# Weight columns in rows of 512: the end of each encoder layer computed by token instead of by feature

## The chip, the cores and the metric

The kernel runs on one core of a Trainium2 chip. Times are device microseconds of one execution; three executions of the kernel before are given with their median. A profile is one execution of its own, with a record of every instruction of the engines: TensorE (PE for its matmuls, PEld for its weight loads), VectorE (DVE), ScalarE (ACT), GpSimd (POOL) and the queue that issues the transfers (SP).

## The reference

A trunk of two layers works on 256 tokens of 1024 features in float32. Each layer computes

```
h = rmsnorm(x, norm_g[l])
proj = h @ w_in[l]                       # inputs of three mixers, their gate paths, 3 x 1024 merge logits
y_a = hgrn2(...) * silu(a_g)             # 1024 wide
y_b = retention(...) * silu(b_g)         # 2048 wide
y_c = rwkv7(...) * silu(c_g)             # 1024 wide
gates = sigmoid(merge)                   # 3 x 1024 per token
mixed = gates[0] * (y_a @ w_branch_a[l]) + gates[1] * (y_b @ w_branch_b[l]) + gates[2] * (y_c @ w_branch_c[l])
x = x + mixed @ w_out[l]
```

and after the last layer a final rmsnorm gives the output. The change concerns the last three lines: merge gates, branch products, output projection. Here they are called the tail of a layer.

## The kernel before, in words

All large products are made in a split form. A weight piece of 128 partitions and 1024 values (512 KB) is loaded (`wr`, in `load_w`), ScalarE casts it to float32r (`wh`, L184), and VectorE takes the difference (`wl`, L187). The other operand has a high and a low part as well (`h_hi` and `h_lo`, `yh` and `yl`, `m_hi` and `m_lo`), and three matmuls stand for one product: high times high, high times low, low times high. `wr`, `wh` and `wl` have three buffers each, which the pieces take in turn.

A block of weights is 1024 rows and 256 columns, which is two pieces. There are two ways to use one:

- `feat_mm` (L200): features on the output's partitions. The stationary operand is a 128 x 128 tile of the weights, the moving one all 256 tokens. A piece holds 128 columns of the block, and 24 matmuls use it.
- `tok_mm` (L210): tokens on the output's partitions. The stationary operand is a 128 x 128 tile of the activations, the moving one 256 weight columns. A piece holds four of the eight k-tiles; the token tile is the outer loop, so both pieces of a block are in use until its second half.

The three mixers come first. Their products are mixed on TensorE with small plain float32 matmuls of the scans (`c_o`, `c_oc`, `b_o`, `b_t` and others). Function `tail` then runs three branches (m = 0, 1, 2 for A, B, C) with four blocks each (b = 0 to 3). For a block, `proj` computes the gate logits into a PSUM bank `pj` (tile `p_mg`), ScalarE and VectorE make the sigmoid in `t_g`, `feat_mm` accumulates the branch product in two half banks of tag `c` (tile `t_o`; branch B takes two weight blocks), VectorE multiplies by the gate (L770), and GpSimd adds to the accumulator `t_acc` (L772). In the last branch the sum is cast to `m_hi` and `m_lo` (L779, L780), with features on the partitions as the output projection needs it for its stationary operand. The output projection, four blocks `wo` by `tok_mm` into `pj`, is added to x (L793), and ScalarE sums the squares for the next norm (L794). `load_y` fetches the mixers' outputs from DRAM through one buffer `yr` and splits them.

The order of the instructions on each engine is written at build time by a planner that simulates the program; instructions of the tail may stand among the last scan's. Each engine's queue runs in that order. PSUM has eight banks: two `pj`, two `c`, two `n`, one `s`, one `ab`.

In SBUF the mixers' tiles lie at bytes 78,848 to 192,000 of a partition (the scan C, with `c_os` as the topmost) and 192,704 to 229,336 (A and B, 35.8 KB). The tail's pool `early` (`t_acc`, `t_g`, `yh0`, `yl0`, `yr`; 34 KB) lies at 194,528 to 229,344, with `t_acc` at its lower end; a tile there waits for the earlier tiles under it.

Of the kernel before, what the change touches and what calls it, by code (L numbers as in the profile page):

```python
# [8 lines left out]
F32 = mybir.dt.float32  # L9
F32R = mybir.dt.float32r  # L10
# [10 lines left out]
NBLK = 93  # L21
WS = (1024, 1024)
TOK = ("ai", "bv", "wo")
# [9 lines left out]
# columns of a layer's packed parameters  # L33
# [9 lines left out]
# columns of the shape constants  # L43
# [9 lines left out]
# of the masks that A takes, and of the rotation that B takes  # L53
# [4 lines left out]
# blocks of weights in a layer, in the order of _blocks()  # L58
# [3 lines left out]
def _blocks():  # L62
    """(key, matrix, row range start, list of (column start, width)) of each block of 1024 rows and 256 columns."""
# [13 lines left out]
    for m in range(3):  # L77
        for b in range(4):
            c = 256 * b
            r.append((("mg", m, b), "w_in", 0, [(15616 + 1024 * m + c, 256)]))  # L80
            for n, w, r0 in ((("wa", "w_branch_a", 0),), (("wb0", "w_branch_b", 0), ("wb1", "w_branch_b", 1024)),
                             (("wc", "w_branch_c", 0),))[m]:
                r.append(((n, b), w, r0, [(c, 256)]))
    for b in range(4):
        r.append((("wo", b), "w_out", 0, [(256 * b, 256)]))
# [3 lines left out]
for _i, _b in enumerate(_blocks()):  # L89
    BK[_b[0]] = _i  # L90
assert len(BK) == NBLK


@with_exitstack
def trunk(ctx: ExitStack, tc, x, wb, pp, lora, cst, gtab, ng, out, parts="ABCT", layers=L, dbg=None):
# [10 lines left out]
    # x and what its norm takes come before the other constants  # L106
# [36 lines left out]
    DP = []  # L143
    for l in range(L):
# [3 lines left out]
        # 1 - mu0 - mu1  # L148
# [7 lines left out]
    # lower bounds: softmax over the layers with its maximum, cumulated, less the first  # L156
# [13 lines left out]
    # cumsum - p[0]  # L170
# [6 lines left out]
    def load_w(l, key):  # L177
        """the parts of a block's halves"""
        W = []
        for h in range(2):  # L180
            raw = ring(wp, [128, 1024], F32, "wr", RW[0], "wr")
            nc.sync.dma_start(raw, wb[2 * (l * NBLK + BK[key]) + h])
            hi = ring(wp, [128, 1024], F32R, "wh", RW[1], "wh")
            S.copy(hi, raw)  # L184
            lo = ring(wp, [128, 1024], F32R, "wl", RW[2], "wl")
            n = WS[h]
            V.tensor_sub(lo[:, 0:n], raw[:, 0:n], hi[:, 0:n].bitcast(F32))  # L187
            if n < 1024:
                G.tensor_sub(lo[:, n:], raw[:, n:], hi[:, n:].bitcast(F32))
            W.append((hi, lo))  # L190
        return W
# [11 lines left out]
    def tok_mm(o, W, t, h):  # L203
        """o[t, column] = h[:, t-tile]^T W; a half of the block holds four k-tiles"""
# [25 lines left out]
    def silu_from(pool, src, shape, tag, tmp, bufs=1, tb=1):  # L230
        """silu of a projection in PSUM"""
# [8 lines left out]
    def norm_T(xs, ss, gb, pool):  # L240
        """xs and the sums of its squares by token; gb: the gains, on every partition"""
# [53 lines left out]
    def c_codes(l, pool):  # L295
# [3 lines left out]
        # tanh(x) = 2 sigmoid(2 x) - 1  # L299
# [5 lines left out]
    def c_prep(l, p, codes, pool):  # L305
        """Everything of pair p up to the chunk products, evacuated and masked."""
# [13 lines left out]
        # normalised kk, negated  # L320
# [8 lines left out]
        # decay and a  # L329
# [21 lines left out]
        # its ninth block holds the stacked identity  # L351
# [4 lines left out]
        # bonus: sum of r k_d r_k over both directions  # L356
# [7 lines left out]
        # k~, beta~, alpha~, r~ of each direction, and the products within its chunks  # L364
# [6 lines left out]
        for d in range(2):  # L371
            # a chunk's blocks of 64: A_rk^T, r~, A_ak, A_rb^T, beta' (first alpha~), A_ab^T, k', diag g, alpha~^T
# [30 lines left out]
    def c_solve(l, p, st, pool):  # L403
        """Inverses of the diagonal 32 x 32 blocks of I - A_ab, one block and every fourth column a partition."""
# [17 lines left out]
        # inverses of the diagonal 4 x 4 blocks, in place: entry (i, k) of block I at 132 I + 32 k + i  # L422
# [27 lines left out]
    def c_scan(l, p, st, pool, ydst):  # L450
# [10 lines left out]
        # v of each direction, transposed  # L461
# [18 lines left out]
        # (I - A_ab)^-1 [A_ak, alpha~^T] by blocks of 32, for a direction's four chunks at a time  # L480
# [14 lines left out]
        # what a chunk makes of its v and of the state before it: mt its output, mk the state after it  # L495
# [19 lines left out]
        # the state from chunk to chunk  # L515
# [24 lines left out]
        # group norm over a head's 64 partitions  # L540
# [14 lines left out]
    # ================= A: HGRN2 =================  # L555
    def a_pair(l, p, pool, ydst):
# [6 lines left out]
        # k = (1 - lb) sigmoid(-x), f = lb + (1 - lb) sigmoid(x); the first layer's lb is p[0] - p[0] = 0  # L563
# [28 lines left out]
    def a_head(l, hd, le, kq, v, g, pool, ydst):  # L592
        # decay sums within 128 positions: forward, and backward negated
# [10 lines left out]
        def pairs(e, s):  # L604
            """K (lower forward, upper backward) and Q (lower backward, upper forward), scaled"""
# [6 lines left out]
        # between the two tiles of 128  # L612
# [30 lines left out]
        # within 8 positions, from their middle  # L643
# [16 lines left out]
        # output, its norm over the 128 partitions and the gate  # L660
# [27 lines left out]
    # ================= B: retention =================  # L688
# [52 lines left out]
    # ================= merge and output =================  # L741
# [10 lines left out]
    def tail(l, ya, yb, yc, x_src, early, pool):  # L752
        acc = [early.tile([128, 2, T], F32, name=f"t_acc{b}") for b in range(4)]
        Y, xs = [], None
        for m in range(3):
            br = ((("wa", 0),), (("wb0", 1), ("wb1", 2)), (("wc", 3),))[m]
            for b in range(4):
# [4 lines left out]
                if b == 0:  # L762
                    Y += [load_y(src, early, pool if m else early, n) for src, n in (((ya, 0),), ((yb[:, 0:8], 1), (yb[:, 8:16], 2)), ((yc, 3),))[m]]
                o = [ps.tile([128, 256], F32, tag="c", bufs=PB["c"], name="t_o") for f in range(2)]
# [180 lines left out]
```

## Time and profile before

| | |
|---|---|
| Runs | 1819.37, 1821.67, 1822.58 us; median 1821.67 |
| Profiled execution | span 1821.9 us from the first to the last instruction; no other time of this execution is recorded |
| Granted TensorE clock, mean | 0.965 |
| Tail of layer 0 | first gate matmul at 695.3 us, last addition of the output projection done at 905.2 us |
| Tail of layer 1 | end at 1821.9 us, with the final norm |
| Weight pieces | 372 transfers of 512 KB, 3.3 us from issue to landing |

A line of the groups reads: source line, engine, operation, output <- inputs, shape, count | busy us, mean ns of one | idle time of the engine just before them, and what ended it. A line of the chain of work reads: start, duration, engine or DMA, output, line, count. A line of the timeline reads: start, duration, engine, line, operation, operands. Durations of matmuls are those of one from start to end and overlap; the distance between starts is what a matmul costs in a stream.

### The profile page before, as it was taken

To read this page: it belongs to the slowest core of one execution; us is meant where nothing else is said; L and a number is where in the kernel's file an instruction comes from. 1 tells how busy PE (TensorE), PEld (TensorE's weight loads), DVE (VectorE), ACT (ScalarE), POOL (GpSimd) and SP (SyncE) were. 2 spreads that over 40 slices of the span, in tenths; PEclk is the share of its full clock that TensorE was granted. 3 is DMA by queue.
4 is the path that set the end of the run, shared out by engine and by line. 5 is a ranking of instruction groups with operands and counts; after the bars stand their busy time and mean duration, and the time that the engine had idled before them with its cause. 6 is when DMAs were issued, how large, how long until landed. Compare 5 with 4: busy or idle time off the path is not lost.

```text
span 1821.9 us, 33791 instructions
## 1 busy us (share of the span) xinstructions
PE 1667.6 (92%) x12960; PEld 1625.0 (89%) x12960; DVE 1415.4 (78%) x2597; ACT 1056.5 (58%) x1940; POOL 322.0 (18%) x312
## 2 busy tenths in 40 slices
PE   6888899999999999999888789988999999999997
PEld 6877899898999998999888788988889999999997
DVE  5799898998878785565657989989998787846554
ACT  5665566757465545555556556757573656456453
POOL 1122222212120200010011222223131202100100
PEclk9989999999999999999988889999999999999999
DMA  6333223324344443755533233233244444437653
GB/s 221 116 118 105 79 96 102 117 86 138 119 155 141 146 148 133 244 200 187 198 114 118 99 100 91 88 109 107 93 133 125 144 142 154 142 131 245 208 186 116
DMA packets 127873, 250.30 MB, mean 137 GB/s; under 512 B 62304, under 2 KB 66784, under 8 KB 127456
## 3 DMA queue, kind: packets, MB, share of 16 engines
q1 hardware_dynamic: 127712, 248.15, 41.6%
q8 instruction: 102, 1.67, 0.4%
q14 instruction: 59, 0.48, 0.1%
HBM read 229.22 MB, written 14.68 MB: 134 GB/s over the span
## 4 chain that ended last, share of the span: by engine, by line
PE 49%; DVE 30%; issue 7%; DMA 6%; ACT 4%; SPq 2%; POOL 0%; DVEq 0%; ACTq 0%; POOLq 0%
PE t_o L200 10%; PE p_mg L200 8%; DVE wl L187 7%; DVE c_tq L439 3%; PE p_bv L210 3%; PE p_vg L200 3%; PE p_bg L200 2%; DMA c_M<-s 2%; PE pj L210 2%; PE c_p L393 2%; DMA s<-c_Z 2%; ACT wh L184 2%; DVE c_ts L441 2%; PE p_rk L200 1%; PE c_p L395 1%
## 5 line engine op out<-in xcount | busy, mean ns | idle before, releaser
L187 DVE TENSOR_TENSOR wl<-wr,wh 128x1024 fp32r<-128x1024 f32 x372 | 475.9, 1280 | 192.3 <-ACT wh L184 190.9
L184 ACT CAST wh<-wr 128x1024 fp32r<-128x1024 f32 x372 | 388.4, 1045 | 272.7 <-PE t_o L200 56.2
L200 PE MATMUL t_o<-yh,wh 128*128 128x256 f32 x512 | 144.7, 284 | 2.8 <-ACT yh L748 2.8
L200 PE MATMUL t_o<-yl,wh 128*128 128x256 f32 x512 | 145.0, 284 | 0.5 <-DVE yl L749 0.5
L200 PE MATMUL t_o<-yh,wl 128*128 128x256 f32 x512 | 144.6, 283 | 0.0
L608 POOL TENSOR_TENSOR a_sl<-a_kq,a_e 128x256 f32<-128x256 f32 x80 | 80.9, 1015 | 230.9 <-ACT a_e L618 66.0
L200 PE MATMUL p_mg<-h_hi,wh 128*128 128x256 f32 x384 | 109.6, 285 | 0.0
L200 PE MATMUL p_mg<-h_hi,wl 128*128 128x256 f32 x384 | 109.4, 285 | 0.0
L200 PE MATMUL p_mg<-h_lo,wh 128*128 128x256 f32 x384 | 108.7, 283 | 0.0
L200 PEld LDWEIGHTS t_o<-yh,wh 128*128 128x128 f32 x512 | 97.6, 191 | 3.2 <-ACT yh L748 3.2
L200 PEld LDWEIGHTS t_o<-yl,wh 128*128 128x128 f32 x512 | 97.9, 191 | 1.0 <-DVE yl L749 0.9
L200 PEld LDWEIGHTS t_o<-yh,wl 128*128 128x128 f32 x512 | 97.9, 191 | 0.0
L393 PE MATMUL c_p<-c_Z,bbd 128*128 128x192 f32 x256 | 68.9, 357 | 29.7 <-DVE bbd L388 25.0
L439 DVE TENSOR_TENSOR c_tq<-W,c_M 128x16 f32<-128x16 f32 (+6 forms) x112 | 89.0, 795 | 1.4
L200 PE MATMUL p_vg<-h_hi,wh 128*128 128x256 f32 x256 | 78.1, 305 | 8.1 <-ACT c_k L288 4.1
L399 ACT COPY c_Z<-c_p 128x192 f32<-128x192 f32 x128 | 40.3, 318 | 74.9 <-DVE c_Z L396 73.7
L200 PE MATMUL p_bg<-h_hi,wl 128*128 128x256 f32 x256 | 75.0, 293 | 4.6 <-DVE wl L187 4.6
L210 PE MATMUL p_bv<-wh,h_hi 128*128 128x256 f32 x256 | 76.1, 297 | 1.1 <-ACT b_z L694 1.1
L210 PE MATMUL p_bv<-wl,h_hi 128*128 128x256 f32 x256 | 75.4, 295 | 1.7 <-DVE wl L187 1.7
L200 PE MATMUL p_vg<-h_lo,wh 128*128 128x256 f32 x256 | 75.8, 296 | 0.0
L200 PE MATMUL p_vg<-h_hi,wl 128*128 128x256 f32 x256 | 75.6, 295 | 0.0
L210 PE MATMUL p_bv<-wh,h_lo 128*128 128x256 f32 x256 | 74.7, 292 | 0.0
(334 smaller groups left out, 5983.3 us busy)
## 6 DMA issues: line engine op xcount, KB each, us to landing
wr<-in_wb_dram SPq DMA_DIRECT2D x372, 512.0 KB, 3.3
c_M<-s SPq DMA_DIRECT2D x64, 128.0 KB, 2.7
c_lt<-in_lora_dram SPq DMA_DIRECT2D x16, 256.0 KB, 2.7
b_sw<-b_z SPq DMA_DIRECT2D x16, 256.0 KB, 3.9
b_gt<-in_gtab_dram SPq DMA_DIRECT2D x16, 256.0 KB, 3.4
yb<-b_y SPq DMA_DIRECT2D x16, 256.0 KB, 3.0
yr<-yb SPq DMA_DIRECT2D x8, 512.0 KB, 5.0
s<-c_Z SPq DMA_DIRECT2D x128, 16.0 KB, 1.9
```

The costliest lines, as they stand in the source:

```text
L184: S.copy(hi, raw)
L187: V.tensor_sub(lo[:, 0:n], raw[:, 0:n], hi[:, 0:n].bitcast(F32))
L200: PE.matmul(o, a[:, k], b[:, k, :], start=(first and n == 0), stop=(last and n == 3 * KT - 1))
L210: PE.matmul(o, a[:, k, t * 128:(t + 1) * 128], b, start=(n == 0), stop=(n == 3 * KT - 1))
L393: PE.matmul(o[:, 2:5], bbd[:, c], z[:, c, 1:8:3], start=True, stop=True)
L395: PE.matmul(o[:, 0:6:5], kbd[:, c], z[:, c, 1:8:6], start=True, stop=True)
L399: S.copy(z[:, c, 4:9:2], o[:, 4:7])
L439: V.tensor_mul(tp, W[:, 0:n, None, 0:j].to_broadcast([128, n, 4, j]), M[:, 0:j, j:j + 4].rearrange("p j i -> p i j")[:, None].to_broadcast ...
L441: V.tensor_reduce(sm, tp, axis=AX.X, op=ALU.add)
L608: G.tensor_mul(s5[:, :, :, 0], k5[:, 0:2, :, 0], e5[:, :, :, 0])
```

## The change

In the tail a block of weights becomes 1024 rows and 512 columns, four pieces of two k-tiles each. The stationary operand of all three products is now a 128 x 128 tile of the activations, the moving one 512 weight columns, and each of the two token tiles has a PSUM bank of its own. Both `pj` banks hold one block of gate logits, both `c` banks one block of a branch product. `t_acc` and `t_g` are by token, 2 x 512 values per partition. The finished sum is transposed on TensorE, four 128 x 128 tiles to a bank of tag `n`, and split into `m_hi` and `m_lo` from there. The number of pieces, transfers, casts and differences stays. The mixers' own products are unchanged. Comments are dropped throughout.

```diff
+    def load_half(l, key, h):
+        raw = ring(wp, [128, 1024], F32, "wr", RW[0], "wr")
+        nc.sync.dma_start(raw, wb[l * NHLF + BK[key] + h])
+        hi = ring(wp, [128, 1024], F32R, "wh", RW[1], "wh")
+        S.copy(hi, raw)
+        lo = ring(wp, [128, 1024], F32R, "wl", RW[2], "wl")
+        V.tensor_sub(lo, raw, hi.bitcast(F32))
+        return hi, lo
...
+    def wide_mm(o, l, key, h, first=True, last=True):
+        hhi, hlo = h
+        for c in range(4):
+            whi, wlo = (w.rearrange("p (k c) -> p k c", c=512) for w in load_half(l, key, c))
+            for i in range(2):
+                k = 2 * c + i
+                for t in range(2):
+                    r = slice(t * 128, (t + 1) * 128)
+                    for n, (a, b) in enumerate(((hhi, whi), (hlo, whi), (hhi, wlo))):
+                        PE.matmul(o[t], a[:, k, r], b[:, i], start=(first and k == 0 and n == 0),
+                                  stop=(last and k == KT - 1 and n == 2))
...
     def tail(l, ya, yb, yc, x_src, early, pool):
-        acc = [early.tile([128, 2, T], F32, name=f"t_acc{b}") for b in range(4)]
+        acc = [early.tile([128, 2, 512], F32, name=f"t_acc{n}") for n in range(2)]
...
-            for b in range(4):
-                o = proj(l, ("mg", m, b))
-                g = early.tile([128, 2, T], F32, tag="t_g", bufs=TG, name="t_g")
-                S.activation(g, o, AF.Exp, scale=-1.0)
+            for n in range(2):
+                o = two("pj", "p_mg")
+                wide_mm(o, l, ("mg", m, n), (h_hi, h_lo))
+                g = early.tile([128, 2, 512], F32, tag="t_g", bufs=TG, name="t_g")
+                for t in range(2):
+                    S.activation(g[:, t], o[t], AF.Exp, scale=-1.0)
                 sigmoid_of_exp(g)
...
-                    W = load_w(l, (key, b))
-                    for f in range(2):
-                        feat_mm(o[f], W, f, Y[y], first=(i == 0), last=(i == len(br) - 1))
-                for f in range(2):
-                    V.tensor_mul((g if m else acc[b])[:, f], o[f], g[:, f])
-                if m:
-                    G.tensor_add(acc[b], acc[b], g)
+                    wide_mm(o, l, (key, n), Y[y], first=(i == 0), last=(i == len(br) - 1))
+                for t in range(2):
+                    V.tensor_mul((g if m else acc[n])[:, t], o[t], g[:, t])
+                    if m:
+                        G.tensor_add(acc[n][:, t], acc[n][:, t], g[:, t])
...
-                    S.copy(m_hi[:, 2 * b:2 * b + 2], acc[b])
-                    V.tensor_sub(m_lo[:, 2 * b:2 * b + 2], acc[b], m_hi[:, 2 * b:2 * b + 2].bitcast(F32))
+                    for t in range(2):
+                        o = ps.tile([128, 4, 128], F32, tag="n", bufs=PB["n"], name="t_t")
+                        for k in range(4):
+                            PE.transpose(o[:, k], acc[n][:, t, 128 * k:128 * k + 128], ident)
+                        hi = m_hi[:, 4 * n:4 * n + 4, 128 * t:128 * t + 128]
+                        S.copy(hi, o)
+                        V.tensor_sub(m_lo[:, 4 * n:4 * n + 4, 128 * t:128 * t + 128], o, hi.bitcast(F32))
...
-        for b in range(4):
-            W = load_w(l, ("wo", b))
-            o = ring(ps, [128, 2, 256], F32, "pj", PB["pj"], "pj")
-            r = slice(256 * b, 256 * b + 256)
-            for t in range(2):
-                tok_mm(o[:, t], W, t, (m_hi, m_lo))
-            for t in range(2):
-                sq = pool.tile([128, 256], F32, tag="t_sq", bufs=2, name="t_sq")
-                V.tensor_add(xs[:, t, r], xs[:, t, r], o[:, t])
-                S.activation(sq, xs[:, t, r], AF.Square, accum_out=s4[:, t, b:b + 1])
+        for n in range(2):
+            o = two("pj", "pj")
+            wide_mm(o, l, ("wo", n), (m_hi, m_lo))
+            r = slice(512 * n, 512 * n + 512)
+            for t in range(2):
+                sq = pool.tile([128, 512], F32, tag="t_sq", bufs=2, name="t_sq")
+                V.tensor_add(xs[:, t, r], xs[:, t, r], o[t])
+                S.activation(sq, xs[:, t, r], AF.Square, accum_out=s4[:, t, n:n + 1])
```

More of the change, by code (lines that the diff above doesn't have):

```diff
@@ L20 @@
 KT = D // 128
-NBLK = 93
-WS = (1024, 1024)
-TOK = ("ai", "bv", "wo")
+NHLF = 186
+TOK = ("ai", "bv")
+WIDE = ("mg", "wa", "wb0", "wb1", "wc", "wo")
 PB = {"pj": 2, "c": 2, "n": 2, "s": 1, "ab": 1}
@@ L77, in _blocks @@
     for m in range(3):
-        for b in range(4):
-            c = 256 * b
-            r.append((("mg", m, b), "w_in", 0, [(15616 + 1024 * m + c, 256)]))
-            for n, w, r0 in ((("wa", "w_branch_a", 0),), (("wb0", "w_branch_b", 0), ("wb1", "w_branch_b", 1024)),
+        for n in range(2):
+            c = 512 * n
+            r.append((("mg", m, n), "w_in", 0, [(15616 + 1024 * m + c, 512)]))
+            for k, w, r0 in ((("wa", "w_branch_a", 0),), (("wb0", "w_branch_b", 0), ("wb1", "w_branch_b", 1024)),
                              (("wc", "w_branch_c", 0),))[m]:
-                r.append(((n, b), w, r0, [(c, 256)]))
-    for b in range(4):
-        r.append((("wo", b), "w_out", 0, [(256 * b, 256)]))
-    return r
-for _i, _b in enumerate(_blocks()):
-    BK[_b[0]] = _i
-assert len(BK) == NBLK
+                r.append(((k, n), w, r0, [(c, 512)]))
+    for n in range(2):
+        r.append((("wo", n), "w_out", 0, [(512 * n, 512)]))
+    return r
+_o = 0
+for _b in _blocks():
+    BK[_b[0]] = _o
+    _o += 4 if _b[0][0] in WIDE else 2
+assert _o == NHLF
 @with_exitstack
@@ L174, in trunk @@
     V.tensor_scalar(omlb, lb, -1.0, 1.0, op0=ALU.mult, op1=ALU.add)
-    def load_w(l, key):
[L179 to L191, printed above, removed]
+    def load_half(l, key, h):
[6 more added lines that the diff above has]
+        return hi, lo
+    def load_w(l, key):
+        return [load_half(l, key, h) for h in range(2)]
+    def wide_mm(o, l, key, h, first=True, last=True):
[9 more added lines that the diff above has]
+                                  stop=(last and k == KT - 1 and n == 2))
     def feat_mm(o, W, f, h, first=True, last=True):
@@ L752, in tail, with two @@
     def tail(l, ya, yb, yc, x_src, early, pool):
-        acc = [early.tile([128, 2, T], F32, name=f"t_acc{b}") for b in range(4)]
+        acc = [early.tile([128, 2, 512], F32, name=f"t_acc{n}") for n in range(2)]
         Y, xs = [], None
+        def two(tag, name):
+            return [ps.tile([128, 512], F32, tag=f"{tag}{t}", bufs=1, name=name) if tag == "pj" else
+                    ps.tile([128, 512], F32, tag=tag, bufs=PB[tag], name=name) for t in range(2)]
         for m in range(3):
@@ L756, in tail @@
             br = ((("wa", 0),), (("wb0", 1), ("wb1", 2)), (("wc", 3),))[m]
-            for b in range(4):
-                o = proj(l, ("mg", m, b))
-                g = early.tile([128, 2, T], F32, tag="t_g", bufs=TG, name="t_g")
-                S.activation(g, o, AF.Exp, scale=-1.0)
+            for n in range(2):
+                o = two("pj", "p_mg")
[3 more added lines that the diff above has]
+                    S.activation(g[:, t], o[t], AF.Exp, scale=-1.0)
@@ L761, in tail @@
                 sigmoid_of_exp(g)
-                if b == 0:
-                    Y += [load_y(src, early, pool if m else early, n) for src, n in (((ya, 0),), ((yb[:, 0:8], 1), (yb[:, 8:16], 2)), ((yc, 3),))[m]]
-                o = [ps.tile([128, 256], F32, tag="c", bufs=PB["c"], name="t_o") for f in range(2)]
+                if n == 0:
+                    Y += [load_y(src, early, pool if m else early, i) for src, i in (((ya, 0),), ((yb[:, 0:8], 1), (yb[:, 8:16], 2)), ((yc, 3),))[m]]
+                o = two("c", "t_o")
@@ L778, in tail @@
                         m_lo = pool.tile([128, KT, T], F32R, name="m_lo")
-                    S.copy(m_hi[:, 2 * b:2 * b + 2], acc[b])
-                    V.tensor_sub(m_lo[:, 2 * b:2 * b + 2], acc[b], m_hi[:, 2 * b:2 * b + 2].bitcast(F32))
-        s4 = pool.tile([128, 2, 4], F32, name="t_s4")
+                    for t in range(2):
[5 more added lines that the diff above has]
+                        V.tensor_sub(m_lo[:, 4 * n:4 * n + 4, 128 * t:128 * t + 128], o, hi.bitcast(F32))
+        s4 = pool.tile([128, 2, 2], F32, name="t_s4")
         ss = pool.tile([128, 2], F32, name="t_ss")
@@ L890, in _pack @@
     a = {k: np.asarray(v) for k, v in inputs.items()}
-    wb = np.empty((L * NBLK, 2, 128, 1024), np.float32)
+    wb = np.empty((L * NHLF, 128, 1024), np.float32)
     for l in range(L):
-        for n, (key, mat, r0, cols) in enumerate(_blocks()):
+        for key, mat, r0, cols in _blocks():
             m = np.concatenate([a[mat][l, r0:r0 + 1024, c0:c0 + w] for c0, w in cols], 1)
+            n = l * NHLF + BK[key]
+            if key[0] in WIDE:
+                wb[n:n + 4] = m.reshape(4, 2, 128, 512).transpose(0, 2, 1, 3).reshape(4, 128, 1024)
+                continue
             if key[0] in TOK:
```

8 lines of the change are left out of this document (4 added, 4 removed).

## The prediction

> **What bounds the kernel now.** First the page's first block and the windows, to see which engine is full in the part that changes (the tail of each layer: gates, branch products, output projection); then the chain of work, to see whether anything but TensorE sets its pace; then the groups, for counts.
>
> ```profile
> PE 1667.6 (92%) x12960; PEld 1625.0 (89%) x12960; DVE 1415.4 (78%) x2597; ACT 1056.5 (58%) x1940; POOL 322.0 (18%) x312
> ...
> 740.00:780.00 40.00, 40.00 (x336) 39.95 (x336) 24.71 (x27) 25.20 (x31) 1.48 (x2) 1.00 0.77 268
> 820.00:860.00 40.00, 40.00 (x335) 40.00 (x335) 23.87 (x26) 20.92 (x25) 3.87 (x3) 1.00 0.52 183
> 880.00:890.00 10.00, 8.74 (x70) 8.33 (x70) 5.54 (x6) 3.62 (x7) 0.83 (x1) 1.00 0.45 158
> ```
>
> A window row reads: length, then busy time and instructions of PE, PEld, DVE, ACT, POOL, then the granted clock, the DMA share, GB/s. From 740 to 880 us TensorE is never idle at full clock, VectorE is at 60%, ScalarE at 52 to 63%. Busy alone doesn't prove a bound, since matmul records overlap; the chain does:
>
> ```profile
> 758.04 5.68 PE t_o L200 x48
> 763.73 5.75 PE p_mg L200 x48
> 769.47 11.52 PE t_o L200 x96
> ...
> 873.15 5.65 PE t_o L200 x47
> 878.83 1.06 ACT wh L184
> 879.91 2.02 DVE wl L187
> 881.97 3.52 PE pj L210 x27
> ```
>
> The chain runs through TensorE alone for 140 us: 96 matmuls in 11.52 us, 120 ns each, block after block. Only the output projection (`pj`) has weight waits on it. So the tail's time is the number of matmuls times their spacing, and the change is about that product. The counts:
>
> ```profile
> L200 PE MATMUL t_o<-yl,wh 128*128 128x256 f32 x512 | 145.0, 284 | 0.5 <-DVE yl L749 0.5
> L200 PE MATMUL p_mg<-h_hi,wh 128*128 128x256 f32 x384 | 109.6, 285 | 0.0
> L210 PE MATMUL pj<-wl,m_hi 128*128 128x256 f32 x128 | 36.6, 286 | 2.5 <-DVE wl L187 2.5
> ```
>
> Each is one of three equal groups: 3 x (512 + 384 + 128) = 3072 matmuls of 256 columns. (The mean of 284 ns is the latency of one; the spacing is 120.) At 120 ns they are 368.6 us of the 1821.9.
>
> **Term 1: 3072 matmuls of 256 columns become 1536 of 512.** The work in columns stays; halved are the instructions and weight loads. The gain therefore hangs on why 256 columns take 120 ns. The timeline, PEld and PE rows in turn:
>
> ```profile
> 788.03 0.19 PEld L200 LDWEIGHTS t_o<-yl,wh 128*128 128x128 f32 x1
> 788.15 0.19 PEld L200 LDWEIGHTS t_o<-yh,wl 128*128 128x128 f32 x1
> ...
> 1788.04 0.28 PE L200 MATMUL t_o<-yh,wh 128*128 128x256 f32 x1
> 1788.16 0.28 PE L200 MATMUL t_o<-yl,wh 128*128 128x256 f32 x1
> ```
>
> Loads and matmuls alternate, both every 120 ns. The chain's rows of the mixers show what other shapes cost (plain float32):
>
> ```profile
> 688.33 0.22 PE c_oc L521 x2
> ...
> 698.47 1.73 PE b_o L718 x8
> ...
> 703.66 0.89 PE c_o L486 x8
> ...
> 706.51 0.44 PE b_t L732 x4
> ```
>
> `c_oc` has 64 columns and costs 0.22 / 2 = 110 ns; `c_o` has 128 and costs 0.89 / 8 = 111; `b_o` has 256 and costs 1.73 / 8 = 216. From 64 to 128 columns nothing is added: the weight load sets a floor of about 111. From 128 to 256 it adds 105, so there the stream sets the time, and the load hides behind it. A plain float32 column takes twice the stream of a float32r one (256 float32r columns take 120, 256 float32 ones 216), so `b_o` is the nearest row to 512 float32r columns with a new weight tile each time: 216. I read 120 as the load's floor, just above the 105 or so that 256 float32r columns need. Bounds for the new matmul: below, 216 (the stream of `b_o`); above, 240, two of today's, if 120 is all streaming; between them, 120 + 105 = 225, if the excess is a fixed sum per instruction. I take 216, since `b_o` has the same alternation of load and stream: 1536 x 216 = 331.8 us, **-36.8**.
>
> The Trainium skill, TensorE: Matmul & The Clock Gate, section Back-to-back issue gap, gives N / 2.4 + 2.5 ns for an isolated warm matmul: 216 at 512 columns, as `b_o`, but 109 at 256, where the trace has 120; by it alone term 1 would be an estimated 1536 x (218 - 216) = 3 us and the time near rival (c)'s. The trace disagrees at 256 columns, and the 120 measured there decides. The same section says that the spacing of load and matmul pairs is set by both operations, which is the reading above and what the trace's floor of 111 bears out.
>
> **Term 2: the transposes.** Sixteen 128x128 transposes a layer, in four groups of four. The row of `b_t` is such a group among other matmuls: 0.44 us with its switches. 8 x 0.44 = **+3.5**. The copies out of them replace the old casts, four of 512 columns a layer before and after:
>
> ```profile
> L253 ACT CAST h_hi<-n_t x8: 586/586/589, 12.8 to 912.9; 128x512 fp32r<-128x512 f32 x8
> L779 ACT CAST m_hi<-t_acc x8: 620/621/622, 846.3 to 1790.5; 128x512 fp32r<-128x512 f32 x8
> L780 DVE TENSOR_TENSOR m_lo<-t_acc,m_hi x8: 677/678/679, 847.3 to 1791.5; 128x512 fp32r<-128x512 f32 x8
> ```
>
> From PSUM 586 against 620: nothing.
>
> **Term 3: the chain from the last branch product to the output projection.**
>
> ```profile
> 1788.60 0.42 DVE L770 TENSOR_TENSOR t_g<-t_o,t_g 128x256 f32<-128x256 f32 x1 [0.29 <-PE t_o L200]
> 1789.19 1.29 POOL L772 TENSOR_TENSOR t_acc<-t_acc,t_g 128x512 f32<-128x512 f32 x1 [10.23 <-DVE t_g L770]
> ```
>
> Today: product, GpSimd add, cast, difference (m_lo starts 1791.5, 0.68 long: 3.6 us in all), hidden by the first matmuls of `pj`. After: two products of 512 columns (0.68 each by the m_lo row), two adds one after the other (2 x 1.29), transposes 0.44, cast 0.59, difference 0.68: 0.68 + 2.58 + 0.44 + 0.59 + 0.68 = 5.0, with semaphores about 5.8 (today 0.6 of the 3.6 are such). The cover is the first half of `wo` block 0, k-tiles 0 to 3, which need only the first 512 columns of the sum: 24 matmuls, 5.2 us. Uncovered 0.5 a layer: **+1**. That holds if TensorE's order has those matmuls before the last transposes; its queue is in order, and if the transposes stand first, it waits for 0.68 + 2.58 = 3.3 us a layer, 6.5 in all. The order on TensorE here already puts later matmuls between the earlier ones' waits (`p_mg` around `c_o`), so I take the small value.
>
> **Term 4: the output projection's waits.** Today its two token tiles each run through both half-blocks, so both halves are released late:
>
> ```profile
> PE pj L210 <- DVE wl L187: 1.3, 2, 0.7
> PE t_o L200 <- ACT yh L748: 1.4, 1, 1.4
> ```
>
> That is 1.3 us a layer. After, each 512 KB piece is used by 12 matmuls and released: **-2.6**. In exchange both `pj` banks belong to one 512-column block, and block 1 waits for block 0's additions. The add of token tile 0 (0.68) runs beside tile 1's last three matmuls (0.65), so about 0.5 a layer: **+1**. At the very end tile 0's add begins 0.65 earlier and both take longer (0.68 against 0.42): nothing.
>
> **Term 5: the start of the tail, beside the last scan.** Three things move. The gates need both `pj` banks at once; one is held until the last `b_pair` has read it:
>
> ```profile
> L236 DVE TENSOR_TENSOR s_g<-p_bg,s_tmp x1: 692/692/692, 699.6 to 699.6; 128x512 f32<-128x512 f32 x1
> 695.54 0.71 PE p_mg L200 x6
> 696.68 1.78 PE p_mg L200 x15
> 740.46 1.06 PE p_mg L200 x9
> 745.73 0.33 SPq L553 DMA_DIRECT2D yc<-c_os  x1
> yc<-c_os SPq DMA_DIRECT2D x16, 128.0 KB, 2.2
> ```
>
> So the 21 matmuls that ran between 695.5 and 698.5 lose their place: 2.5 us. Against that, one gate block is now 48 x 216 = 10.4 us of filler instead of 5.8, beside the 1.4 us in which TensorE waited for `yh` and others like it. Third, `t_g` grows from 2 to 4 KB in three buffers; the pool `early` from 34 to 40 KB, downward. It lay within the 35.8 KB that A and B had left; now the first accumulator reaches under the last scan's tiles, `c_os` the last of them, free when the store issued at 745.7 lands (2.2 us). Today two gate blocks and two products are done by 740, when the third gate block starts; so the first 512 block's product is due there and may wait some 8 us, with a gate block (10.4 us) in between as cover, provided that VectorE's queue has the weight differences ahead of it. I take **+1** a layer for the three, between -1.5 (filler wins) and +5 (VectorE is blocked): **+2**.
>
> **Term 6: the weight feed.** The pieces, 512 KB each, are the same 372, on SP's queue in nearly the same order; `load_y` follows four pieces instead of two. TensorE takes one in 12 x 216 = 2.6 us instead of 2.88. A buffer's round is landing, cast, difference:
>
> ```profile
> wr<-in_wb_dram SPq DMA_DIRECT2D x372, 512.0 KB, 3.3
> L187 DVE TENSOR_TENSOR wl<-wr,wh 128x1024 fp32r<-128x1024 f32 x50 | 66.4, 1329 | 46.2 <-ACT wh L184 46.1
> L184 ACT CAST wh<-wr 128x1024 fp32r<-128x1024 f32 x51 | 53.4, 1048 | 56.4 <-PE t_o L200 28.0 <-PE p_mg L200 24.4 <-DMA wr<-in_wb_dram 4.0
> ```
>
> 3.3 + 1.05 + 1.33 = 5.7 over three buffers is 1.9 a piece, under 2.6, and the casts wait for TensorE, not it for them. Where `yb` is read as well, 268 GB/s become some 295 at a share of 0.85: **+1** for that. ScalarE's and VectorE's sigmoid work is the same elements in half the instructions, off the path.
>
> **Sum.** -36.8 + 3.5 + 1 - 2.6 + 1 + 2 + 1 = -30.9. The profiled span of 1821.9 lies 0.2 above the median of the runs (1821.67); 1821.9 - 30.9 = **1791**.
>
> **Rivals.** (a) *A fixed sum per instruction*: 225 ns a matmul, 345.6 us, 14 more: **1805**. For it: no float32r row of another width; against it: `b_o` has no such excess over the stream. (b) *New waits*: transposes ahead of `wo` (+5.5) and the first accumulator blocking VectorE (+8): between 1796 and 1805, say **1802**. For it: in-order queues and both banks taken at once; against it: the slack of a gate block. (c) *The other side: float32r streams at 120 ns per 256 columns*. Then 512 cost 240, term 1 is nothing, and the new work remains: 1821.9 + 5.9 = **1828**. It decides from (368.6 - 5.9) / 1536 = 236 ns a matmul upward. For it: 120 is above both the floor of 111 and the stream of 105. Against it: blocks with pauses run below 120, as this one, at 2.02 / 17 = 119, and a stream bound would not give back.
>
> ```profile
> 725.32 2.02 PE t_o L200 x17
> ```
>
> (d) *The price is per instruction*, whatever the columns: 1536 x 120, a gain of 184: **1643**. Against it: `c_o` to `b_o`, where columns double and so does the price. The Trainium skill, in the section named, gives about 131 ns as the sustained spacing at 512 columns; by it 1536 x 131 would be an estimated gain of 167. The trace bears out nothing of that. (e) *The planner's new order disturbs the scans* and eats the gain: **1818**.
>
> **Chances.** Forecast 0.60 (own range 1783 to 1798), (a) 0.14, (b) 0.13, (c) 0.08, (d) 0.01, (e) 0.04. 1783 to 1810 holds the forecast's cases and (a) and (b) but for their tails. 0.2% (3.6 us) is about what a measurement tells from no change: faster 0.88, same 0.03, slower 0.09.
>
> **What would show it.** Right: groups of `t_o` x256, `p_mg` x192, `pj` x64 with 128x512, and 48 of them in 10.4 us on the chain; `pj` waits for VectorE gone; four transposes at 0.44. 10.8 means (a), 11.5 means (c). A gap of 3 us before the transposes or one near 740 to 748 means (b). The prediction falls if the spacing is over 225 or TensorE's idle time in the tail grows by more than 5 us a layer.

## The result, and the profile after

The change made the kernel slower: 1849.18 us median (four runs, 1844.83 to 1854.19) against 1820.52 for the kernel before in the same session (1815.17 to 1822.58), a ratio of 1.0166 with a 95% interval of 1.0141 to 1.0192. The forecast was 1791 with a range up to 1810; the error is 58 us. The profiled execution took 1854.19 us with a span of 1852.4; a span is 1.7 to 2.4 us, mostly 1.8, shorter than the time of its execution in every run here that has both.

First the stretches that the prediction argued from, by the windows of both kernels: from the first gate matmul to the last matmul of the output projection, layer 0 and layer 1. Columns: window, length, busy time and count of PE, PEld, DVE, ACT, POOL, granted clock, DMA share, GB/s. Before:

```profile
695.30:903.73 208.43, 203.89 (x1687) 202.10 (x1685) 120.49 (x145) 111.99 (x155) 15.53 (x13) 1.00 0.56 192
1605.37:1813.35 207.98, 203.46 (x1685) 201.77 (x1683) 118.74 (x143) 109.13 (x151) 15.54 (x13) 1.00 0.53 181
```

After:

```profile
698.07:918.43 220.36, 202.41 (x935) 165.63 (x933) 115.59 (x124) 107.89 (x135) 18.43 (x13) 0.96 0.58 181
1624.41:1843.83 219.42, 201.35 (x933) 164.05 (x930) 113.07 (x122) 105.13 (x131) 18.35 (x13) 0.97 0.54 172
```

The two tails together went from 416.4 to 439.8 us, +23.4. (The whole profiled execution is 30.5 us longer; the other 7.1 us lie outside the tails, and what they are due to is not shown.) Length less PE's busy time is idle TensorE: 4.5 us a layer before, 18 after. Where it is idle, and for what, stands in TensorE's waits of layer 0's tail:

```profile
PE t_o L202 <- ACT yh L760: 11.0, 1, 11.0
...
PE c_ox L517 <- ACT qp L514: 2.2, 2, 1.3
```

One wait of 11.0 us, for the high part of `ya`. The chain of work of after, at that place and then in the steady part (start, duration, what):

```profile
734.90 0.71 PE c_gn L557 x2
...
738.53 0.73 POOL c_os L564
739.27 0.33 SPq L565
739.65 5.74 DMA yr<-ya
...
795.16 21.76 PE t_o L202 x96
816.92 10.88 PE p_mg L202 x48
...
877.22 0.44 PE t_t L800 x4
...
894.04 5.44 PE pj L202 x24
899.48 0.89 PE t_t L800 x8
900.37 1.22 DVE wl L186
901.59 0.61 DVE m_lo L803
```

Two things are to be read here. First, the chain runs from the scan's last normalisation over the store of `yc` (L565) straight into the first load of `ya`: the whole tail hangs behind the scan. From there to 791.6, where rows are left out, the chain is the eight loads of `load_y`, one after another through the one buffer `yr`, each with its cast and difference; from 746.6 to 791.0 TensorE is busy beside them for all but 0.6 us. Second, the new stream: 96 matmuls in 21.76 us, 48 in 10.88, that is 227 ns each, where the forecast took 216. The queue that issues transfers, in the kernel before:

```profile
710.29 0.42 SPq L747 DMA_DIRECT2D yr<-ya  x1
718.69 0.32 SPq L747 DMA_DIRECT2D yr<-ya  x1
724.65 0.32 SPq L747 DMA_DIRECT2D yr<-yb  x1
745.73 0.33 SPq L553 DMA_DIRECT2D yc<-c_os  x1
750.34 0.33 SPq L747 DMA_DIRECT2D yr<-yb  x1
```

and after:

```profile
704.20 0.33 SPq L565 DMA_DIRECT2D yc<-c_os  x1
739.27 0.33 SPq L565 DMA_DIRECT2D yc<-c_os  x1
739.65 0.42 SPq L759 DMA_DIRECT2D yr<-ya  x1
```

Before, three loads go out ahead of the last store of `yc`, and branch A's products fill TensorE beside the last scan. After, the first goes out behind that store, 29 us later. Between the first gate matmul and 735.6 us, TensorE had two gate blocks and 60 product matmuls of 256 columns to put beside the scan in the kernel before, and has one gate block (48 matmuls of 512 columns) and no product in after. The rest of what used to fill the scan's pauses is still to be done when it ends.

### The profile page after: what moved, and what is told of

It is laid out like the page before. It is cut to its first block, busy times and chain, and to the rows that moved or that the text cites. A ratio compares the mean times of both kernels' runs of the same rounds, so it can differ in the third digit from the quotient of the medians.

```text
span 1852.4 us, 30668 instructions
## 1 busy us (share of the span) xinstructions
PE 1662.5 (90%) x11456; PEld 1548.0 (84%) x11456; DVE 1407.7 (76%) x2553; ACT 1048.7 (57%) x1900; POOL 324.2 (18%) x312
## 4 chain that ended last, share of the span: by engine, by line
PE 43%; DVE 32%; DMA 10%; issue 7%; ACT 5%; SPq 2%; POOL 1%; DVEq 0%; ACTq 0%; POOLq 0%
PE t_o L202 7%; DVE wl L186 7%; PE p_mg L202 5%; PE p_bv L222 3%; DVE c_tq L451 3%; PE p_vg L212 2%; PE pj L202 2%; PE p_bg L212 2%; DMA c_M<-s 2%; PE p_rk L212 2%; DMA yr<-yb 2%; DVE c_ts L453 2%; PE c_p L405 2%; DMA s<-c_Z 1%; ACT wh L184 1%
## 5 line engine op out<-in xcount | busy, mean ns | idle before, releaser
L202 PE MATMUL t_o<-wh,yh 128*128 128x512 f32 x256 | 101.1, 398 | 21.3 <-ACT yh L760 21.3
L202 PE MATMUL t_o<-wh,yl 128*128 128x512 f32 x256 | 101.6, 397 | 0.1
L202 PE MATMUL t_o<-wl,yh 128*128 128x512 f32 x256 | 92.2, 395 | 0.0
L790 POOL TENSOR_TENSOR t_acc<-t_acc,t_g 128x512 f32<-128x512 f32 x16 | 28.2, 1788 | 289.4 <-DMA wr<-in_wb_dram 156.5
L202 PE MATMUL p_mg<-wh,h_hi 128*128 128x512 f32 x192 | 75.8, 395 | 2.4 <-ACT wh L184 2.4
L202 PEld LDWEIGHTS t_o<-wh,yh 128*128 128x128 f32 x256 | 48.7, 191 | 32.5 <-ACT yh L760 22.1
L202 PE MATMUL p_mg<-wh,h_lo 128*128 128x512 f32 x192 | 75.2, 391 | 0.0
L212 PE MATMUL p_bg<-h_lo,wh 128*128 128x256 f32 x256 | 74.9, 292 | 0.0
L212 PE MATMUL p_bg<-h_hi,wh 128*128 128x256 f32 x256 | 74.6, 292 | 0.0
L212 PE MATMUL p_rk<-h_hi,wh 128*128 128x256 f32 x256 | 74.5, 291 | 0.0
```

The source lines that it names most:

```text
L202: PE.matmul(o[t], a[:, k, r], b[:, i], start=(first and k == 0 and n == 0), stop=(last and k == KT - 1 and n == 2))
L212: PE.matmul(o, a[:, k], b[:, k, :], start=(first and n == 0), stop=(last and n == 3 * KT - 1))
L790: G.tensor_add(acc[n][:, t], acc[n][:, t], g[:, t])
```

## The experiments

Each kernel was timed beside the kernel before. The time is the median; the ratio is against the kernel before, with its interval. "Tails" is the sum of the two tails' lengths, "idle" the part of it without a busy TensorE, both from window rows like those above, of one profiled execution. Where the granted clock is lowered, the busy part is longer for it. In e8, e10 and e11 something of the computation is left out, as their expectations say.

| Kernel | Time, us | Ratio | Tails, us | Idle, us |
|---|---|---|---|---|
| before | 1820.2 to 1820.9 | | 416.4 | 9.1 |
| after | 1849.18 | 1.0166 (1.0141 to 1.0192) | 439.8 | 36.0 |
| e1: second accumulator moved | 1828.19 | 1.0046 (1.0030 to 1.0062) | 421.0 | 19.6 |
| e2: before with a pool of 40 KB | 1861.73 | 1.0221 (1.0195 to 1.0248) | 451.8 | 34.7 |
| e3: accumulators swapped | 1840.13 | 1.0109 (1.0075 to 1.0143) | 434.8 | 32.7 |
| e4: only the output projection wide | 1816.69 | 0.9975 (0.9959 to 0.9990) | 412.3 | 7.1 |
| e5: e1 with two raw buffers, two gate buffers | 1830.11 | 1.0050 (1.0035 to 1.0066) | 421.9 | 19.6 |
| e6: both accumulators moved, two raw buffers | 1838.00 | 1.0094 (1.0071 to 1.0118) | 427.2 | 24.1 |
| e7: before with two raw buffers, two gate buffers | 1826.72 | 1.0039 (1.0024 to 1.0055) | 416.9 | 8.0 |
| e8: e1, each matmul split to 256 | 1816.70 | 0.9987 (0.9970 to 1.0003) | 412.4 | 3.4 |
| e9: mixed, branch A narrow | 1817.41 | 0.9984 (0.9970 to 0.9998) | 408.3 | 9.7 |
| e10: e9 without transposes | 1806.89 | 0.9927 (0.9909 to 0.9945) | 403.8 | 7.7 |
| e11: only branch A wide | 1826.31 | 1.0033 (1.0017 to 1.0050) | 421.4 | 10.1 |

### The reach of the pool: e1, e2, e3

Theory M: the pool `early` grew from 34 to 40 KB and now begins at 188,384, so that its lowest tile, the first accumulator, lies over tiles of the scan (which end at 192,000). The accumulator must wait for them, and the planner then puts the loads behind the scan's last store. e1 takes 4 KB out of `early`; the rest ends above the scan:

```diff
-        acc = [early.tile([128, 2, 512], F32, name=f"t_acc{n}") for n in range(2)]
+        acc = [(early, pool)[n].tile([128, 2, 512], F32, name=f"t_acc{n}") for n in range(2)]
```

> The changed kernel with one of its two accumulators (t_acc1, 4 KB) moved from the pool `early` to the tail's other pool; nothing else differs. `early` is then 36 KB and no longer reaches under the last scan's tiles. Theory M (memory: the lower end of `early` under the scan's tiles makes the planner hold back the whole start of the tail): the first load of ya is issued near 712 us instead of 739.7, the 11 us wait of t_o for yh shrinks to under 3, and with 1536 matmuls at 227 ns instead of 3072 at 120 (-20) and some 6 us of new work the time is 1820.5 - 14 = about 1806, range 1798 to 1814. Rival B (banks: both PSUM banks taken at once and a block twice as long leave TensorE without other work beside the scan): the wait stays, and the time is that of the changed kernel, 1849, at most 5 us less.

e2 puts the harm into the kernel before, with its tiling untouched, by nothing but buffers that are not needed:

```diff
-TG, YR = 3, 1
+TG, YR = 6, 1
```

> The kernel before with six buffers for t_g instead of three (12 KB, as the changed kernel has for it); nothing else differs, and the three more buffers are not needed. Its pool `early` is then 40 KB, as in the changed kernel, and lies under the last scan's tiles as there. Theory M: the first load of ya is issued only after the last store of yc, near 740 us, and TensorE waits for yh as in the changed kernel: +15 to +25 us a layer, 1850 to 1870. Rival B: no 512-column block and no pair of banks is here, so the time stays within 4 us of 1820.5.

e3 leaves the pool at 40 KB and puts the second accumulator, which is needed later, at its lower end:

```diff
-        acc = [early.tile([128, 2, 512], F32, name=f"t_acc{n}") for n in range(2)]
+        acc = [early.tile([128, 2, 512], F32, name=f"t_acc{1 - n}") for n in range(2)][::-1]
```

> The changed kernel with the two accumulators exchanged in the pool: the one that lies under the scan's tiles is now that of the second 512 columns, first written some 20 us later, when the scan's last tile is free. Theory M in the form W (the first write to the accumulator waits for the scan's tiles): the wait is gone, 1806 to 1815. Theory M in the form O (the planner gives the pool's tiles out in program order and holds back all later ones behind the one that has to wait, whichever is written first): as the changed kernel, 1849 within 5 us.

e2 shows that M is real: 41 us slower. (Three more gate buffers come with the larger pool; that they do harm by themselves is not tested apart from it.) Its waits and its transfer queue are those of after:

```profile
PE t_o L200 <- ACT yh L748: 11.9, 2, 10.4
...
728.28 0.33 SPq L553 DMA_DIRECT2D yc<-c_os  x1
728.66 0.42 SPq L747 DMA_DIRECT2D yr<-ya  x1
```

e1 takes back 21 of after's 28.7 us, and its first load goes out at 708.4 again; but it ends 7 us behind the kernel before, not 14 ahead as M alone forecast. e3 keeps the late load (issued at 728.97, right behind the store at 728.60) and a wait of 10.3 us for `yh`, though the tile that reaches into the scan's memory is not written before the second product: so what delays the loads is the order that the planner writes, not a wait of the first product. That is form O, but its time is not: e3 is 9 us faster than after, where O allowed 5. 5 of the 9 us are in the tails, and no run shows why.

### What is left: e5, e6, e7

In e1 the first block of branch B took 29.7 us for its 96 matmuls, against 21.8 in the stream. 3.4 us of that TensorE is idle; the granted clock is 0.89 there. The window:

```profile
771.30:801.00 29.70, 26.30 (x96) 19.69 (x97) 13.63 (x12) 12.58 (x13) 0.00 (x0) 0.89 0.72 250
```

Theory L took the late loads of `yb` through the one raw buffer for the cause. e5 and e6 give them two, in a pool of 36 KB (e5 with `TG` 2, e6 with both accumulators moved); e7 does the same to the kernel before.

```diff
-TG, YR = 3, 1
+TG, YR = 2, 2
```

> The changed kernel with its second accumulator in the other pool (as in the first remedy, 1828.19 us), two gate buffers instead of three and two raw buffers for the branch inputs instead of one: the early pool is 36 KB, from 192480, clear of what the scan holds. Theory L (late loads): in the first remedy the four loads of branch B went through one raw buffer, were issued from 773.0 us on, and the first block of branch B took 29.65 us instead of 21.53, that is 8.1 us a layer; with two raw buffers two of them go out ahead of the yc store, so the block returns to 21.5 and the time to 1828 - 16 = 1812 (1808 to 1816). Rival N (the 8 us by which the first remedy is slower than the kernel before belong to the wide form itself, its longer fillers in the scan): the block stays long or the loss appears elsewhere, 1824 to 1832.

> The changed kernel with both accumulators in the other pool, three gate buffers and two raw buffers: again 36 KB for the early pool, from 192480. By theory L the loads come as early as with two gate buffers, and the time is 1812 (1808 to 1816). The first product writes an accumulator that now lies in memory of the scan, so it waits for the scan's end; by theory A (the first accumulator is a wait of its own) the accumulation bank of the first product stays occupied and TensorE stands for it: 3 to 5 us a layer more than with two gate buffers, 1818 to 1822.

> The kernel before with two gate buffers and two raw buffers (36 KB, clear of the scan): what the remedy does without the change. In the kernel before TensorE stands 4.5 us a layer in the whole tail, so at most 9 us can be had. By theory L, by which the late loads are a thing of the changed kernel, the time stays within 1815 to 1821. If the second raw buffer is a gain of its own in any tiling: 1806 to 1812, and then what it brings to the changed kernel says nothing of the change.

Theory L fell: e5 is no faster than e1, and lands in the range of its rival N. Its two loads of `yb` do go out at 723, but their casts (ScalarE's rows of e5, behind the scan's last write of `c_os`) come only at 776.7:

```profile
772.01 0.60 ACT L561 ACTIVATE c_os<-c_os,pp 128x256 f32<-128x256 f32 x1 [0.81 <-DVE c_os L559]
776.68 2.00 ACT L760 CAST yh<-yr 128x1024 fp32r<-128x1024 f32 x2
```

The parts of `yb` (`load_y` with `pool`) lie in memory that the scan holds. In the kernel before, e1 and e5 this cast starts 2.3 us after the issue of the last `yc` store (745.73 to 747.98, 767.83 to 770.18, 774.33 to 776.68). So the question became why the scan ends so late. e6 missed its forecast time, but is 8 us slower than e5, as its theory A said (6 to 10) of a first accumulator in the scan's memory: in each layer TensorE waits 2.1 us for `t_acc` and 2.7 for `wh`, where e5 has no wait for `t_acc` and at most 0.5 for `wh`. e7 was 6.5 us slower than the kernel before with the same tails, which its expectation had not allowed for (see the end of the next part).

### The filler in the scan: e8, e11, e9

What stands between two steps of the scan on TensorE (its matmuls `c_oc` to `c_gn`, then `c_gn` to `c_gn`, by windows; the counts take in an edge). Before:

```profile
734.56:738.10 3.54, 3.54 (x32) 3.54 (x32) 1.53 (x4) 2.26 (x3) 0.00 (x0) 1.00 0.46 148
738.70:741.35 2.65, 2.65 (x24) 2.65 (x24) 1.14 (x2) 1.36 (x2) 0.00 (x0) 1.00 0.37 119
```

e1:

```profile
751.90:757.40 5.50, 5.50 (x25) 4.43 (x24) 1.91 (x3) 1.52 (x2) 0.00 (x0) 1.00 0.36 109
757.85:762.60 4.75, 4.75 (x22) 3.94 (x21) 2.45 (x2) 1.56 (x3) 0.00 (x0) 1.00 0.63 208
```

By the timeline, 31 and 24 narrow matmuls stand in these two places before, and 26 and 21 wide ones in e1: nearly as many, though a wide one costs 1.9 times as much on the chip (227 against 120 ns). The scan's next step waits for them: in e1 `c_os` is written at 752.58 and `c_gn`, which reads it, starts at 757.42, 4.8 us later, with TensorE busy all the while; before, it is 735.67 and 738.09, 2.4 us. That is theory P. Why the planner places so many is not shown; it orders them as if a wide one cost little more than a narrow one. e8 splits every wide matmul of e1 into two:

```diff
-                        PE.matmul(o[t], a[:, k, r], b[:, i], start=(first and k == 0 and n == 0),
-                                  stop=(last and k == KT - 1 and n == 2))
+                        for j in range(2):
+                            q = slice(256 * j, 256 * j + 256)
+                            PE.matmul(o[t][:, q], a[:, k, r], b[:, i, q], start=True,
+                                      stop=True)
```

> The first remedy (1828.19 us) with each matmul of 512 columns as two of 256 columns on the same weights and bank, each with start and stop, so that the accumulation over the blocks is left out; loads, casts, vector work and order stay. It weighs term 1 by itself: 1536 instructions become 3072. By a fixed part of 13 ns in each instruction (120 = 106.7 + 13.3 and 227 = 213.3 + 13.3) the stream grows by 1536 x 13.3 = 20 us: 1848 (1843 to 1852). By the columns alone (the rest of the spacing being the feed): 1828 (1825 to 1832). By a price per instruction: far above 1860.

e11 does so for everything but branch A, the filler:

> The reverse of the mixed kernel: the first remedy with only branch A in wide matmuls; in branches B, C and the last projection each is two of 256 columns on the same weights and bank, each with start and stop, which leaves out the accumulation there. By theory P the scan is stretched as in the first remedy (its end near 763 us, branch B's first block stalled), and the stream pays 2 x 576 x 13.3 ns on top: 1843 (1838 to 1848), slower than the kernel split throughout (1816.7) though it has fewer instructions. By rival N the harm goes with the wide matmuls of B, C and the last projection, and it is the split kernel less 2 x 192 x 13.3 ns: 1812 (1808 to 1816).

e9 is a whole kernel: branch A by token in blocks of 256 columns, everything behind it wide.

```diff
+        for b in range(4):
+            o = proj(l, ("mg", 0, b), tok=True)
...
+            W = load_w(l, ("wa", b))
+            for t in range(2):
+                tok_mm(o[:, t], W, t, Y[0])
+            q = 256 * (b % 2)
+            V.tensor_mul(acc[b // 2][:, :, q:q + 256], o, g)
-        for m in range(3):
+        for m in (1, 2):
```

> The first remedy (1828.19 us) with branch A, whose matmuls fill the last scan, in blocks of 256 columns by token (four gate blocks and four product blocks), and branches B, C and the last projection in the wide form. It computes everything. Theory P (the planner puts about as many matmuls between two steps of the scan whether they have 256 or 512 columns, 24 in the kernel split to 256 columns and 21 to 25 in the first remedy, so wide ones stretch the scan from about 742 to 763 us, and what waits for the memory of the scan, the parts of yb, comes late): the scan ends near 742, the first block of branch B takes 21.5 us, and against the split kernel (1816.7) 2 x 576 wide matmuls save 13.3 ns each for each instruction less, 15.3 us: 1801 (1797 to 1806). Rival N (wide matmuls cost the 8 us that the first remedy is behind by in some way of their own, wherever they run): 1815 to 1828.

e8 missed its forecast by 31 us and said the most. The price in the stream is as forecast; its chain has the narrow price again, 23.04 for what takes 21.76 in wide matmuls:

```profile
735.80 2.92 PE p_mg L204 x24
738.72 0.43 PE c_gn L556 x2
739.15 2.86 PE p_mg L204 x24
742.02 0.43 PE c_gn L559 x2
...
769.83 23.04 PE t_o L204 x192
```

Over 3072 instructions instead of 1536 that is +20 us. Yet the kernel became 11.5 us faster than e1, since the scan ended at 742 instead of 763, with 24 matmuls between its steps once more, but of 2.9 us; TensorE's idle time fell from 19.6 to 3.4 us. So the wide matmuls cost e1 its gain as filler of the scan, not in the stream, and they cost more than the gain. (In e8 each matmul also starts and stops by itself; e9 below accumulates as usual and has the early end of the scan too.) e11 puts the late scan back with branch A alone, and has both kinds of filler: 24 wide and 2 narrow matmuls before the first `c_gn` take 6.1 us, 25 narrow ones before the second take 3.4, where e1's 21 wide ones take 5.2. In e11 `c_gn` ends at 764.5 in layer 0 (in layer 1 the scan is stretched about half as much), the tails are 421.4 as in e1, and the time is 9.6 us over e8's although it has 384 matmuls fewer. Its forecast by P, 1843, was still 17 too high, and its time lies between those of P and of N: by the prices, its stream of branches B, C and the projection is 15.3 us longer than e1's; TensorE's busy time rose by 9.8 us and its idle time fell by 9.4, from 19.6 to 10.1. A likely reason, not tested: a stall that ends at a fixed time is not made later by more work ahead of it.

In e9 the scan ends at 740 and branch B's first block loses nothing:

```profile
775.81:797.70 21.89, 21.89 (x97) 17.91 (x97) 14.04 (x13) 13.54 (x16) 0.00 (x0) 1.00 0.70 234
```

Its tails are the shortest of any kernel that computes everything, 8.1 us under those before. Its time, 1817.41, is 2.9 us under (ratio 0.9984, 0.9970 to 0.9998), not the 19 that P forecast, and lies in the range of rival N (1815 to 1828), though e1's stall is gone from branch B's first block, whose matmuls are wide. P's forecast started from e8 and took 15.3 us off it; e9's tails are only 4.0 us shorter than e8's. Of the difference some 6 us are idle time, 9.7 against e8's 3.4: branch A's blocks run by token tile with both pieces in use to the end, which may be the reason (in layer 0 TensorE waits there 1.6 us for `yh` and 0.8 for `wl`, and in e8 for neither) and was not tested. The rest is not accounted for.

By the medians, 5 of the 8.1 us that the tails lost do not arrive in the time. By the profiles, all do: the spans are 1821.9 before and 1813.7 in e9, 8.2 us apart, and the mixers of both layers take 1371.9 and 1372.3. But the profiled execution of the kernel before was a long one, about 1823.7 us with the 1.8 added, 3.4 over the 1820.3 of e9's session, and that of e9, 1815.49, was 1.9 under its median. Single executions of the kernel before went from 1813.0 to 1826.2 in that session, so the 5 us can't be placed.

What the mixers add or take therefore stays open. Layer 0's, whose matmuls write the same tiles in the same order in all kernels here, took 673 to 683 us in the profiled executions. Layer 1's took 686 to 697, in several orders, but the order alone does not set the time: e4, e7, e10 and e11 have the same one, and it took 688, 696, 686 and 688 us. e7, with the tails of before, is slower by 6.5 us, and no run shows why.

### The smaller terms: e10, e4

e10 takes the transposes out of e9.

> The mixed kernel without its transposes: the parts of the sum are taken from it by token, as it stands, so the last projection multiplies the wrong side of it; everything else stays. It weighs terms 2 and 3. By the prediction's terms (transposes 3.5 us, chain from the last product to the last projection 1): 4.5 us less than the mixed kernel (3 to 6). By the row of the first remedy's trace (16 transposes take 2.26 us a layer with 0.52 of idle time in it): 4.5 too. If the transposes stand beside other waits: 0 to 1 less. If the wait for the sum's last columns, four transposes with two casts and two subtractions between them, was dearer than the trace shows: over 7.

The tails fell by 4.6 us, the prediction's sum of terms 2 and 3 (4.5). The time fell by 10.5. The rest goes with layer 1's mixers: 693.2 us in e9, 685.6 in e10 (the same window in layer 0 is 679.1 and 680.8):

```profile
907.80:1601.02 693.22, 626.38 (x4781) 606.83 (x4781) 584.82 (x1151) 411.49 (x802) 144.09 (x141) 0.96 0.38 118
...
906.71:1592.34 685.63, 621.11 (x4779) 602.72 (x4779) 580.24 (x1151) 411.81 (x804) 146.50 (x142) 0.97 0.38 118
```

The planner wrote another order for layer 1 here than in e9. It is also e7's, though, where the same stretch took 695.7 us, so the order is not shown to be the cause. The gain of e10 beyond its tails stays open.

e4 is the kernel before with only the output projection in the new form (no transposes are needed there, since the sum is by feature).

> The kernel before with the output projection alone in the new form: 512 weight columns moving, each token tile with a bank of its own, 192 matmuls instead of 384 over both layers. Gates, branch products and the cast of the sum stay by feature, without transposes. With 227 ns a matmul against 2 x 120 the stream gives -2.5 us, the released weight pieces give the 1.3 us a layer of waits back, the shared banks cost 0.5 to 1 a layer: 1820.5 - 4 = 1816, range 1813 to 1820. If the new form itself did the harm (rival B), this is slower than before: above 1822.

It came out as forecast, and its tails are 4.1 us shorter: 384 x 120 - 192 x 227 = 2.5 are stream by the measured spacing, and 1.6 are the prediction's term 4, 4.1 together.

## Why the prediction was wrong, by its own steps

**Term 5, the start of the tail, is the step that failed.** It named the right place: the pool grows downward, the first accumulator reaches under the scan's tiles, `c_os` last. It then priced it as a wait of one product with a gate block of 10.4 us as cover: +1 a layer, +5 at most. But the accumulator is allocated ahead of the loads in the program, and the planner ordered the loads behind the store that ends the scan (739.65 behind 739.27 us). What lost its start was not a product but all of branch A, the filler of the last scan. e1 against after: 18.7 us of tails, 21 of time; e2 against before, with nothing changed but the gate buffers: 35.4 and 41. The sign of the second half of this term was wrong too: a longer gate block as filler was booked as a gain, and e8 and e11 show that wide filler stretches the scan and delays branch B. The prediction had that kind of thing as rival (e), at 1818 and a chance of 0.04, and had no kernel in mind where it would cost more than the gain. Rival (b)'s sign, a gap near 740 to 748, came as well (735.6 to 746.6), but not by its mechanism: TensorE waited for `yh`, not for a VectorE that the accumulator blocked.

**Term 1 was mis-sized.** 1536 x 227 = 348.7 against 368.6 is -20, not -36.8: rival (a), a fixed sum per instruction, had 225 and was right on the spacing (48 matmuls in 10.88 us, where 10.8 was its sign). Taking `b_o` as the nearest row gave the stream without that sum. The two measured widths give 106.7 ns for each 256 columns and 13.3 for each instruction: 120 = 106.7 + 13.3 and 227 = 213.3 + 13.3. Two widths always allow such a split, and no third was run; e8, with 120 ns for 256 columns by token, shows that the narrow price does not come from the old way of using the weights. The Trainium skill, TensorE: Matmul & The Clock Gate, section Back-to-back issue gap, gives 216 ns at 512 columns by its formula for an isolated matmul and about 131 as the sustained spacing; here 227 was measured, so neither holds for this pair of float32r load and matmul.

**Terms 2, 3 and 4 held, near enough.** The transposes cost 0.44 + 0.44 + 0.89 a layer, 3.5 in all. Of term 3's branches the cheap one came: 24 matmuls of `pj` stand ahead of the last transposes, and TensorE then waits 0.5 us for `m_hi` and 0.4 for `m_lo`, 1.8 over both layers against +1, though GpSimd's adds took 1.79 us in the median instead of 1.29. Term 4's waits for `wl` in the output projection are gone (e4). **Term 6**, +1: no wait for a weight piece shows in the chain from 795 to 894 us, but just ahead of it TensorE waits 1.2 us for `wh` and 0.3 for `wl` (1.3 and 0.5 in layer 1), behind the late loads. e1, whose loads go out early, has none of these waits in layer 0.

The prediction's own tests told it: the spacing is over 225, and idle time in the tail grew by 13.5 us a layer, where 5 was the bound. With term 1 at its measured size and term 5 out of the way the sum would have been about 1807 (1821.9 - 20 + 3.5 + 1.8 - 1.6 + 1). So of the error of 58 us some 16 go to term 1 and the terms beside it, and some 42 to the start of the tail. Moving the accumulator (e1) takes back 21 of the 42. The other 21 were still missing in e1. e9, with narrow matmuls beside the scan, came to 1817: 11 of the 21 are back, and some 5 are the price of its 384 more instructions (384 x 13.3 ns). What the last 5 are stays open; no kernel here came to 1807 with the whole of the work done. (The prediction also set the profiled span beside the median of the times as if they were one measure, which hides 1.8 us, and showed weight loads at 788 us and matmuls at 1788 us as alternating; both have the 120 ns. Neither changes the outcome.)

## What to carry to other kernels

When a tile grows, compute the new bounds of its pool and see whose memory they now overlap: price an overlap not by the one tile that waits but by everything that an ordering planner will place behind it. Before an instruction is made wider, ask what it fills: between the steps of a serial chain the number of instructions may stay while each takes twice as long, and the chain's end moves with it. Put the wide form where TensorE is full anyway, and keep the narrow one beside the scan, as e9 does; the gain there was 8.1 us of the tails and 2.9 us of the time.

## What was not expected of the hardware

The prediction had no term for the clock. A gap lowered it for a while in after. Windows of the 11 us of idle TensorE and what follows:

```profile
735.60:746.60 11.00, 0.04 (x1) 0.04 (x1) 1.63 (x3) 4.64 (x8) 1.45 (x2) 0.55 0.55 155
...
746.60:748.60 2.00, 1.96 (x4) 1.14 (x5) 1.17 (x1) 0.87 (x1) 0.00 (x0) 0.50 0.64 262
748.60:750.60 2.00, 2.00 (x7) 1.56 (x6) 0.00 (x0) 0.00 (x0) 0.00 (x0) 0.54 0.86 236
750.60:752.60 2.00, 2.00 (x10) 1.59 (x9) 0.00 (x0) 1.05 (x2) 0.00 (x0) 1.00 0.07 29
```

The granted clock is 0.50 for the first 2 us of work and 0.54 for the next; then it is full again. The rows of the timeline give the price of the first matmuls:

```profile
748.42 0.63 PE L202 MATMUL t_o<-wl,yh 128*128 128x512 f32 x1
748.84 0.63 PE L202 MATMUL t_o<-wh,yl 128*128 128x512 f32 x1
749.27 0.63 PE L202 MATMUL t_o<-wl,yh 128*128 128x512 f32 x1
```

They start 427 ns apart (the first three distances are 592 to 668), against 227 at full clock. Eight slow ones cost 2.1 us on top of the gap. And 427 is twice 213.3 with nothing added: the 13 ns that the two widths at full clock leave for each instruction do not show at half clock.
